# Two chained transformer blocks on one core: norms by halves, projection columns held on chip, eight buffers for raw weights

## The chip, the cores and the metric

The kernel runs on one core of a Trainium2 chip. The time is device microseconds of one execution; three runs of the kernel before took 1541.4 us in the median (1539.8 to 1542.86). Everything is one launch of a program of 23,433 instructions, without loops at run time.

## What is computed

Two blocks in a row on 256 tokens of width 1024 (`x`), the first with 256 context tokens beside them (`ctx`). The first block has two layers:

```
h  = rms(x)*g_pre*(1+sc1) + sh1 ;  hc likewise from ctx
u, uc = h @ w_in, hc @ w_in            # latent attention, short conv, bidirectional SSD scan
x  = x + g1 * rms(y @ w_out)*g_post     # y: the three mixers side by side
h2 = rms(x)*g_pre_ffn*(1+sc2) + sh2
x  = x + g2 * rms(relu(h2 @ w_ff1)**2 @ w_ff2)*g_post_ffn
# layer 0 does the last three lines for ctx too; layer 1 for x alone
```

The factors sh, sc, g come from `silu(c) @ w_mod`. The second block has two layers, one with dilated windowed attention (mixer a), one with a sliding window and sinks (mixer b):

```
h = mixer(x)                            # ends in  (o * silu(z)) @ w_out
x = layer_norm(sqrt(2)*x + h) * ln_g + ln_b
x = x + sigmoid(x @ ple_w_gate) * (p @ ple_w_proj)
```

All products are wanted in float32 accuracy.

## The kernel before

Tokens lie in four tiles of 128: tiles 2 and 3 are x (`X`), 0 and 1 the context (`CTX`). A tile `xt[t]` is two halves of 128x512. Every product is split by hand into float32r parts: an operand is a pair (high, low), and `mm3` issues three matmuls for each of the K blocks of 128 (high·high, high·low, low·high). A product of a token tile with 512 columns and K = 1024 is thus 24 matmuls of 128x512.

Weights come from memory block by block in `wblk` (L170): SP fetches 512 KB (two K blocks of 512 columns) into one of the five buffers of the ring `raw`; then `split` (L225) makes the pair, ACT by a cast (L226), DVE by a subtraction (L227), each on 128x512. The pairs lie in the rings `wh` and `wl` (ten slots each, so one block of eight K steps and two steps more), or, for the last `keep` K steps of a block, in two tiles of the general ring `u` (41 slots of 128x512, in which activations, layer outputs and x^T pairs lie too). A raw buffer comes free when its split is done.

Norms: `normed` (L400) squares each half of a tile on ACT with an accumulator, `rpow` (L164) takes the power -1/2 in two instructions on GpSimd (an add, L167, and a power, L168), and DVE scales both halves (L410). `modulated` (L414) then takes, for each of the eight K steps, PE transposes into a PSUM tile (two of those exist), a scale and shift on DVE (L424), an ACT cast of its result (L226) and a subtraction on DVE or GpSimd (L227). `postnorm` (L427) is the norm after a projection: square and gate product for each half once both halves are there, `rpow`, and x += on DVE (L435).

Order: the framework takes the instructions in the order of the program as their rank, plays a model of the engines, and lets each engine take the ready instruction with the best rank; `tc.high_priority(offset=n)` (and `sooner(n)`, L136) lifts what is inside by n ranks. So each engine has one fixed queue in the end, and the queues were interleaved by the model's times. All semaphores are made by the framework.

The stages, in order of time: the start with the first modulation; `mix(0)`; `out_projection(0)` (L881), which does the left 512 columns for all four tiles, then the right ones for X, the norm chain of X, then the right ones and the chain of CTX; `ffn(0)` (L903), eight steps of 512 hidden columns, of which the last is by token for X; `mix(1)`; `out_projection(1)`, x alone, with a chain for each tile; `ffn(1)`; `mixer_a`; `second(0)` (L1231): output projection by columns, layer norm and transposes by tiles (L1247), gate products; `mixer_b`; `second(1)`. `done` is the function by which each of these starts the norm and the modulation of what comes next; it does both at once. `load_cols(1)`, the masks and the rope tables of the second block are fetched by DMAs that GpSimd issues.

Of the kernel before, what the change touches and what calls it, by code (L numbers as in the profile page):

```python
# [16 lines left out]
P = 128  # L17
# [47 lines left out]
def body(ctx, tc, A, out):  # L65
# [8 lines left out]
    raw, wh, wl = pool("raw", 5), pool("wh", 10), pool("wl", 10)  # L74
# [89 lines left out]
    def rpow(out, a, b, eps):  # L164

        w = out.shape[1]
        POOL.tensor_scalar(out, a, eps if b is None else b, None if b is None else eps, ALU.add, *(() if b is None else (ALU.add,)))  # L167
        POOL.tensor_tensor(out, out, mhalf[:, 0:w], ALU.pow)  # L168
# [258 lines left out]
    def postnorm(t, halves, gate):  # L427

        s2, rs, r = S(2), S(1), [R(), R()]
        for hf in range(2):  # L430
            ACT.activation(R(), halves[hf], AF.Square, scale=1.0 / 32, accum_out=s2[:, hf:hf + 1])
            (DVE if hf else POOL).tensor_tensor(r[hf], halves[hf], gate[hf], ALU.mult)
        rpow(rs, s2[:, 0:1], s2[:, 1:2], EPS)
        for hf in range(2):
            DVE.scalar_tensor_tensor(xt[t][hf], r[hf], rs, xt[t][hf], ALU.mult, ALU.add)  # L435
# [44 lines left out]
    def mix(i, hT, W1, step):  # L480
# [389 lines left out]

        wuq = wsmall(A["w_uq"][i], 384, 2)
# [3 lines left out]
        if step is not None:  # L875
            parts["m"] = mods()
        interleaved(parts, "piiiilpdiiiiiiiseeeclcsccllssssazagzaga" if last
# [3 lines left out]
    def out_projection(i, ytok, done):  # L881

        gate = {r: mod_gate(i, 2, O_GQM, r) for r in ((0,) if i == 1 else (0, 1))}
        W = wblk(A["w_out"][i], [(0, 512)])
        if i == 0:
            for t in CTX:
                xt[t] = [U(), U()]
                load_x(t, SP)
        first = {}
        for t in X + (() if i else CTX):  # L890
            ps = AN()
            mm3(ps, list(zip(ytok(t), W)))
            first[t] = U()
            ACT.copy(first[t], ps)
        W = wblk(A["w_out"][i], [(512, 512)])
        for pair in ((X[0:1], X[1:2]) if i else (X, CTX)):
            for t in pair:
                ps = AN()
                mm3(ps, list(zip(ytok(t), W)))
                postnorm(t, [first[t], ps], gate[0 if t >= 2 else 1])  # L900
            done(pair)

    def ffn(i, h2, h2x, h2c, step, done):  # L903
# [3 lines left out]
        gate = {r: mod_gate(i, 5, O_GQF, r) for r in ((0,) if last else (0, 1))}  # L907
        for r_ in range(8):
            if r_ == 0 and last:

                nb = 2
                Ws = [wblk(A["w_ff1"][i], [(512 * q, 512)], keep=KT if q else 0) for q in range(nb)]
                first = {(t, q): (U(F32R), U(F32R)) for t in range(2) for q in range(nb)}
                for t in range(2):
                    for q in range(nb):
# [8 lines left out]
                        split(tp, *first[t, q])  # L924
            if last and r_ < nb:
# [15 lines left out]
            for (a, b), src in zip(parts, srcs):  # L941
                for ft in range(4):
# [8 lines left out]
                    if r_:  # L951
                        step(2)
            W7 = [wblk(A["w_ff2"][i], [(512 * n, 512)], 4 * r_, 4) for n in range(2)]
            for pair in (pairs if r_ == 7 else (sum(pairs, ()),)):
                by_token = r_ == 7 and pair == X
                for t, n in [(t, n) for t in pair for n in range(2)] if by_token else [(t, n) for n in range(2) for t in pair]:
# [8 lines left out]
                    else:  # L965
                        DVE.tensor_tensor(acc[t, n], acc[t, n], ps, ALU.add)
                    if r_ == 7 and n == 1:
                        postnorm(t, [acc[t, 0], acc[t, 1]], gate[0 if t >= 2 else 1])
                if r_ == 7:
                    done(pair)  # L970
# [22 lines left out]
    def xT():  # L993
# [3 lines left out]
        def fill(t):  # L997
            for j, pair in enumerate(tiles):
# [5 lines left out]
                split(tp[:, 0:256].rearrange("p (q c) -> p q c", q=2), h, l)  # L1004
# [14 lines left out]
    def load_mask(n):  # L1019
        m = C([P, 5, 256], "c_mask", BF16, tag="c_tri")[:, 0:4, :].rearrange("p (s a) c -> p s (a c)", s=2)  # L1020
        for s in range(2):
            r = R()
            POOL.dma_start(r, A[n][:, s * 512:(s + 1) * 512])
# [207 lines left out]
    def second(i, oT, pp, fill, done):  # L1231
        w_out = A["a_w_out_2" if i == 0 else "b_w_out_2"][0]
        lg, lb = [U(), U()], [U(), U()]
# [3 lines left out]
        st = [S(12), S(12)]  # L1237
        hT, transpose = xT()
        for n in range(2):
            W = wblk(w_out, [(512 * n, 512)])  # L1240
            for t in range(2):
                x = xt[2 + t]
                ps = AN()
                mm3(ps, tok(oT, t, W))
                DVE.scalar_tensor_tensor(x[n], x[n], ALPHA, ps, ALU.mult, ALU.add)
                DVE.bn_stats(st[t][:, 6 * n:6 * n + 6], x[n])
        for t in range(2):  # L1247
            x = xt[2 + t]
            mv, rs = S(2), S(1)
            DVE.bn_aggr(mv, st[t])  # L1250
            rpow(rs, mv[:, 1:2], None, LN_EPS)
            for n in range(2):
                DVE.scalar_tensor_tensor(x[n], x[n], mv[:, 0:1], lg[n], ALU.subtract, ALU.mult)
                DVE.scalar_tensor_tensor(x[n], x[n], rs, lb[n], ALU.mult, ALU.add)
            transpose(t)
        W = [wblk(A["ple_w_gate_2"][i], [(512 * n, 512)], keep=(0 if n else KT)) for n in range(2)]
        got = None
        for t in range(2):
            x = xt[2 + t]
            for n in range(2):  # L1260
# [3 lines left out]
                ACT.activation(e, ps, AF.Tanh, scale=0.5)  # L1264
                DVE.scalar_tensor_tensor(e, e, 1.0, pp[t][n], ALU.add, ALU.mult)
                DVE.tensor_tensor(x[n], x[n], e, ALU.add)
                if i == 1:
                    SP.dma_start(out[0, t * P:(t + 1) * P, 512 * n:512 * n + 512], x[n])
            done(t)
            if t == 0:  # L1270
                got = fill()
        return got
# [97 lines left out]
```

## Time and profile before

| | before |
|---|---|
| median of 3 runs | 1541.4 us |
| profiled execution, its own time | 1537.98 us |
| its span, first to last instruction | 1535.9 us |
| mean granted TensorE clock | 0.986 |
| HBM read | 233.87 MB, 153 GB/s over the span |

The profile is that of one execution. Matmuls are pipelined, so their busy time (PE) is not the same as PE at its peak; the pace of back-to-back matmuls is read from the chain of waits. PEclk is the granted clock of TensorE as a share of 2.4 GHz; its two levels are 1.2 and 2.4 GHz. "<-" behind an idle time names what ended it.

### The profile page before, as it was taken

How to read it: one execution, taken by the hardware profiler on the slowest of the kernel's cores; microseconds unless marked ns; L12 is line 12 of the kernel's file. 1: busy time of each engine (PE TensorE's matmuls, PEld its weight loads, DVE VectorE, ACT ScalarE, POOL GpSimd, SP SyncE). 2: the span in 40 equal slices, each digit the busy share in tenths (PEclk: the TensorE clock that was granted, in tenths of full speed). 3: DMA queues.
4: the chain of work that ended last, by engine and by line, in shares of the span. 5: the costliest groups of instructions: out<-in, count | busy, mean ns of one | idle time of the engine just before them, and what ended most of it. 6: DMA issues, size and time to landing. Idle time of an engine off the chain costs nothing.

```text
span 1535.9 us, 23433 instructions
## 1 busy us (share of the span) xinstructions
PE 1470.2 (96%) x8417; PEld 1215.3 (79%) x8417; DVE 1036.4 (67%) x2057; ACT 740.4 (48%) x1594; POOL 308.2 (20%) x356
## 2 busy tenths in 40 slices
PE   6997999999999999998899899999999999999998
PEld 4766678888878888878797689997888889878886
DVE  3559556478597557478776756676876786567866
ACT  3433345564233333255556654565566457445663
POOL 1225201150001111034331301112310320021110
PEclk9998999999999999999999999999999999999999
DMA  9854622325366546334423546555436550645442
GB/s 294 266 182 153 219 84 88 97 66 195 123 219 206 180 152 200 109 83 135 132 76 117 165 139 213 188 195 169 153 107 203 162 179 15 219 139 180 138 149 69
DMA packets 131687, 236.51 MB, mean 154 GB/s; under 512 B 12624, under 2 KB 31251, under 8 KB 131571
## 3 DMA queue, kind: packets, MB, share of 16 engines
q1 hardware_dynamic: 130688, 233.46, 47.0%
q0 software_dynamic: 704, 1.50, 0.3%
q8 instruction: 66, 1.08, 0.3%
q14 instruction: 50, 0.41, 0.1%
q10 hardware_dynamic: 179, 0.06, 0.0%
HBM read 233.87 MB, written 1.11 MB: 153 GB/s over the span
## 4 chain that ended last, share of the span: by engine, by line
PE 84%; DVE 7%; DMA 4%; issue 2%; ACT 2%; POOL 1%; SPq 0%; ACTq 0%; DVEq 0%; POOLq 0%
PE sc L212 47%; PE mm L212 20%; PE tp L459 3%; DVE wl L227 2%; PE fl L303 2%; DMA raw<-in_w_mod_dram 1%; DMA raw<-in_ple_w_gate_dram 1%; PE fl L212 1%; DMA raw<-in_w_in_dram 1%; PE sc L793 1%; PE mm L639 1%; PE sc L1083 1%; PE sc L634 1%; DVE u L782 1%; PE sc L1108 1%
## 5 line engine op out<-in xcount | busy, mean ns | idle before, releaser
L227 DVE TENSOR_TENSOR wl<-raw,wh 128x512 fp32r<-128x512 f32 (+1 forms) x606 | 421.2, 731 | 141.1 <-ACT wh L226 138.1
L226 ACT CAST wh<-raw 128x512 fp32r<-128x512 f32 (+1 forms) x606 | 359.2, 620 | 307.0 <-PE sc L212 104.5
L212 PE MATMUL sc<-wh,u 128*128 128x512 f32 (+2 forms) x1424 | 458.6, 389 | 3.5 <-DVE r L505 2.0
L212 PEld LDWEIGHTS sc<-wh,u 128*128 128x128 f32 x1424 | 265.4, 189 | 58.8 <-ACT p L226 2.2
L212 PE MATMUL sc<-wl,u 128*128 128x512 f32 (+2 forms) x712 | 274.6, 387 | 0.1
L212 PE MATMUL sc<-u,wh 128*128 128x256 f32 (+1 forms) x1072 | 265.1, 336 | 1.8 <-ACT wh L226 1.1
L212 PE MATMUL mm<-wh,u 128*128 128x512 f32 (+1 forms) x648 | 219.3, 395 | 1.0 <-ACT u L226 1.0
L212 PEld LDWEIGHTS sc<-u,wh 128*128 128x128 f32 x1072 | 184.0, 191 | 24.5 <-issue 2.0
L212 PE MATMUL sc<-u,wl 128*128 128x256 f32 (+1 forms) x536 | 178.0, 335 | 0.0
L212 PEld LDWEIGHTS sc<-wl,u 128*128 128x128 f32 x712 | 134.6, 189 | 24.8 <-DVE wl L227 0.5
L949 POOL TENSOR_TENSOR r<-r 128x256 f32<-128x256 f32 (+1 forms) x60 | 64.3, 1073 | 420.1 <-ACT r L947 380.2
L212 PEld LDWEIGHTS mm<-wh,u 128*128 128x128 f32 x648 | 122.2, 190 | 26.1 <-ACT u L226 1.7
L212 PE MATMUL mm<-wl,u 128*128 128x512 f32 (+1 forms) x324 | 127.2, 393 | 0.0
L212 PE MATMUL mm<-u,wh 128*128 128x256 f32 (+1 forms) x512 | 117.6, 317 | 1.1 <-ACT wh L226 1.0
L212 PEld LDWEIGHTS sc<-u,wl 128*128 128x128 f32 x536 | 102.0, 191 | 9.6
L342 DVE SCALAR_TENSOR_TENSOR q<-raw,c_sT,q 128x512 f32<-128x512 f32 x112 | 85.0, 788 | 13.8 <-DMA raw<-in_w_mod_dram 13.2
L212 PEld LDWEIGHTS mm<-u,wh 128*128 128x128 f32 x512 | 86.1, 191 | 9.2 <-issue 1.7
L212 PE MATMUL mm<-u,wl 128*128 128x256 f32 (+1 forms) x256 | 80.4, 314 | 0.0
L950 DVE TENSOR_TENSOR u<-r,u 128x256 fp32r<-128x256 f32 (+1 forms) x60 | 33.6, 561 | 63.0 <-POOL r L949 60.7
L1016 POOL TENSOR_TENSOR r<-r,r 128x512 f32<-128x512 f32 (+1 forms) x30 | 44.6, 1491 | 151.4 <-DVE r L1014 151.3
L212 PEld LDWEIGHTS mm<-wl,u 128*128 128x128 f32 x324 | 61.5, 190 | 12.5 <-issue 0.8
L227 POOL TENSOR_TENSOR u<-r,u 128x256 fp32r<-128x256 f32 (+1 forms) x48 | 38.2, 801 | 119.3 <-ACT u L226 119.0
(318 smaller groups left out, 1984.7 us busy)
## 6 DMA issues: line engine op xcount, KB each, us to landing
raw<-in_w_ff_dram SPq DMA_DIRECT2D x128, 512.0 KB, 4.5
raw<-in_w_mod_dram SPq DMA_DIRECT2D x80, 512.0 KB, 4.5
raw<-in_a_w_in_dram SPq DMA_DIRECT2D x80, 512.0 KB, 3.9
raw<-in_w_in_dram SPq DMA_DIRECT2D x32, 512.0 KB, 5.1
raw<-in_b_w_in_dram SPq DMA_DIRECT2D x18, 512.0 KB, 4.6
raw<-in_w_mod_dram SPq DMA_DIRECT2D x32, 256.0 KB, 5.2
raw<-in_w_out_dram SPq DMA_DIRECT2D x16, 512.0 KB, 3.8
raw<-in_ple_w_gate_dram SPq DMA_DIRECT2D x16, 512.0 KB, 3.9
```

Of the source, the lines that this page charges most:

```text
L212: PE.matmul(ps, s, m, start=(i == 0), stop=(i == n - 1))
L226: ACT.copy(h, src)
L227: (eng or DVE).tensor_tensor(l, src, f(h), ALU.subtract)
L303: PE.matmul(ps[32 * g:32 * g + 32, :], sT[:, k + q, :], rs[g // per][:, q, w * (g % per):w * (g % per) + w], start=(k + q == 0), stop=(k + ...
L342: DVE.scalar_tensor_tensor(a, r[:, q, :], w, a, ALU.mult, ALU.add)
L459: PE.transpose(tp[:, b * P:(b + 1) * P], p[:, b * P:(b + 1) * P], ident)
L634: PE.matmul(ps[:, b * P:(b + 1) * P], qT[t][:, hs], kT[b][:, hs], start=True, stop=True, skip_group_check=True)
L639: PE.matmul(po[64 * e:64 * e + 64, hp * P:(hp + 1) * P], V[b // 2][:, 256 * (b % 2) + 64 * h:256 * (b % 2) + 64 * h + 64], pT[e][:, b * P: ...
L782: DVE.tensor_scalar(o, o, cs[:, t, c:c + 1], 0.0, ALU.subtract, ALU.min)
L949: POOL.tensor_tensor(f2[:, a:b], r[:, a:b], r[:, a:b], ALU.mult)
L950: DVE.tensor_tensor(l, f2[:, a:b], f(h), ALU.subtract)
L1016: POOL.tensor_tensor(a[:, 0:w], a[:, 0:w], b[:, 0:w], ALU.add)
```

## The change

- `raw` has eight buffers, not five. The scratch for DMAs issued by GpSimd is cut to 1024 bytes; all DMAs that GpSimd issued (`load_cols(1)`, masks, rope tables) are issued by ACT.
- `rpow` does its add on DVE; the power stays on GpSimd.
- `modulated`: ACT makes the high part itself from PSUM (scale and shift in the activation), beside DVE's float32 result; both and the subtraction are lifted by 300.
- `postnorm` is a function that is called for each half as it comes, lifted by 300. In `out_projection` it reads the product in PSUM, so the copy of the left halves (L894) is gone.
- `done` now starts the norm alone and gives back a function that does the modulation; the callers run it later: X's after CTX's products, CTX's inside `ffn`'s first step, or in `mix(1)` between the projections of X and of CTX (part "m"); in layer 1, that of tile 3 after tile 2's first products in `ffn(1)`.
- `out_projection(1)`, `ffn(1)` and `second` go tile by tile over both column blocks, in the order (0,1) for the first tile and (1,0) for the second; one block lies in `u` (keep=KT), one in `wh` and `wl`.
- `second`: layer norm chain lifted by 300, transposes moved behind the projections of both tiles; ln_g and ln_b lie in the ring `q`; `ple(1)` is issued whole after the first tile's gates.

```diff
-    raw, wh, wl = pool("raw", 5), pool("wh", 10), pool("wl", 10)
+    raw, wh, wl = pool("raw", 8), pool("wh", 10), pool("wl", 10)
@@ rpow
-        POOL.tensor_scalar(out, a, eps if b is None else b, ...
+        DVE.tensor_scalar(out, a, eps if b is None else b, ...
         POOL.tensor_tensor(out, out, mhalf[:, 0:w], ALU.pow)
@@ modulated
-            DVE.tensor_scalar(r[:, 0:w], tp[:, 0:w], a, b, ALU.mult, ALU.add)
-            split(r[:, 0:w], h, l, POOL if k % 2 else DVE)
+            with tc.high_priority(offset=300):
+                ACT.activation(h, tp[:, 0:w], AF.Identity, bias=b, scale=a)
+                DVE.tensor_scalar(r[:, 0:w], tp[:, 0:w], a, b, ALU.mult, ALU.add)
+                (POOL if k % 2 else DVE).tensor_tensor(l, r[:, 0:w], f(h), ALU.subtract)
@@ postnorm
+    def postnorm(t, gate):
+        s2, rs, r = S(2), S(1), {}
+        @sooner(300)
+        def half(hf, src, o, eng):
+            r[hf] = o
+            ACT.activation(R(), src, AF.Square, scale=1.0 / 32, accum_out=s2[:, hf:hf + 1])
+            eng.tensor_tensor(o, src, gate[hf], ALU.mult)
+            if len(r) == 2:
+                rpow(rs, s2[:, 0:1], s2[:, 1:2], EPS)
+                for q in range(2):
+                    DVE.scalar_tensor_tensor(xt[t][q], r[q], rs, xt[t][q], ALU.mult, ALU.add)
+        return half
@@ out_projection
+        W.append(wblk(A["w_out"][i], [(512, 512)], keep=KT if i else 0))
+        half = {t: postnorm(t, gate[0 if t >= 2 else 1]) for t in X + (() if i else CTX)}
+        end = None
+        def product(t, n):
+            ps = AN()
+            mm3(ps, list(zip(ytok(t), W[n])))
+            half[t](n, ps, U(), DVE)
+        if i == 0:
+            for t in X + CTX:
+                product(t, 0)
         for pair in ((X[0:1], X[1:2]) if i else (X, CTX)):
             for t in pair:
+                for n in (1,) if i == 0 else (1, 0) if end else (0, 1):
+                    product(t, n)
+            new = done(pair)
+            if end:
+                end()
+            end = new
+        return end
@@ ffn
-                Ws = [wblk(A["w_ff1"][i], [(512 * q, 512)], keep=KT if q else 0) for q in range(nb)]
+                Ws = [wblk(A["w_ff1"][i], [(512 * q, 512)], keep=0 if q else KT) for q in range(nb)]
...
-                    for q in range(nb):
+                    for q in (1, 0) if t else (0, 1):
...
+                    if t == 0:
+                        end()
...
+                if r_ == 0 and src is h2x and not last:
+                    end()
...
+                    with tc.high_priority(offset=300 if r_ == 7 else 0):
                         DVE.tensor_tensor(acc[t, n], acc[t, n], ps, ALU.add)
+                    if r_ == 7:
+                        if n == 0:
+                            half[t] = postnorm(t, gate[0 if t >= 2 else 1])
+                        half[t](n, acc[t, n], R(), DVE if n else POOL)
                 if r_ == 7:
-                    done(pair)
+                    new = done(pair)
+                    if later:
+                        later()
+                    later = new
+        return later
@@ mix: "piiiilpdiiii..." becomes "piiiilmpdiiii...", in layer 1 "m" is the function given back by ffn(0)
@@ second
+        W = [wblk(w_out, [(512 * n, 512)], keep=KT if n else 0) for n in range(2)]
+        lg, lb = [Q(), Q()], [Q(), Q()]
...
         for t in range(2):
             x = xt[2 + t]
+            for n in (1, 0) if t else (0, 1):
+                ps = AN()
+                mm3(ps, tok(oT, t, W[n]))
+                with tc.high_priority(offset=300):
+                    DVE.scalar_tensor_tensor(x[n], x[n], ALPHA, ps, ALU.mult, ALU.add)
+                    DVE.bn_stats(st[t][:, 6 * n:6 * n + 6], x[n])
             ...                       # bn_aggr, rpow, 4 scalar_tensor_tensor, lifted by 300
         W = [wblk(A["ple_w_gate_2"][i], [(512 * n, 512)], keep=(0 if n else KT)) for n in range(2)]
         for t in range(2):
+            transpose(t)
+            for n in (1, 0) if t else (0, 1):
...
@@ body
     def mid0(pair):
-        modulated(normed(pair), ...)
+        xn = normed(pair)
+        return lambda: modulated(xn, ...)
-    pp = second(0, oT, pp, late, transpose)
+    pp = second(0, oT, pp, lambda: ple(1)(), transpose)
```

## Rows read from the trace of the kernel before

**Rows 1.** The page: busy us of each engine, share, instructions

```profile
PE 1470.2 (96%) x8417; PEld 1215.3 (79%) x8417; DVE 1036.4 (67%) x2057; ACT 740.4 (48%) x1594; POOL 308.2 (20%) x356
```

**Rows 2.** Windows: stretch, width, busy by engine (count), granted clock, DMA share, GB/s

```profile
335.00:655.00 320.00, 319.91 (x1438) 258.89 (x1437) 214.10 (x337) 109.22 (x192) 38.64 (x31) 1.00 0.52 169
320.00:330.00 10.00, 6.74 (x38) 5.26 (x37) 8.00 (x18) 4.28 (x12) 4.31 (x7) 0.83 0.00 0
675.00:685.00 10.00, 7.60 (x38) 5.65 (x38) 8.37 (x16) 2.56 (x7) 2.35 (x3) 1.00 0.42 104
695.00:715.00 20.00, 16.33 (x106) 14.39 (x104) 17.44 (x43) 11.96 (x34) 9.07 (x12) 0.91 0.61 184
850.00:870.00 20.00, 14.51 (x56) 10.03 (x56) 15.80 (x34) 11.26 (x30) 8.09 (x11) 0.91 0.41 129
1045.00:1055.00 10.00, 7.57 (x28) 5.54 (x27) 6.91 (x11) 4.34 (x11) 6.77 (x9) 0.86 0.50 158
1370.00:1380.00 10.00, 6.59 (x30) 4.34 (x29) 8.99 (x19) 4.37 (x10) 3.12 (x5) 1.00 0.42 139
1500.00:1510.00 10.00, 8.56 (x33) 6.27 (x32) 8.80 (x17) 3.19 (x8) 3.40 (x4) 0.83 0.34 105
100.00:150.00 50.00, 39.98 (x242) 28.70 (x236) 42.10 (x112) 18.84 (x45) 31.30 (x39) 0.86 0.53 175
```

**Rows 3.** Waits of PE: total us, times, longest

```profile
PE tp L420 <- DVE q L410: 7.0, 4, 3.2
PE fl L303 <- DMA raw<-in_w_mod_dram: 3.8, 5, 2.0
```

**Rows 4.** Chain of waits, 355 to 380 us: start, length, what

```profile
363.04 10.88 PE sc L212 x48
```

**Rows 5.** Timeline around the first layer's output projection: start, length, what

```profile
306.57 0.40 PE L212 MATMUL sc<-wh,u 128*128 128x512 f32 x1
311.64 0.63 ACT L431 ACTIVATE r<-u 128x512 f32<-128x512 f32 x1
322.53 0.88 DVE L410 TENSOR_SCALAR q<-u,s 128x512 f32<-128x512 f32 x2 [0.69 <-POOL s L168]
```

**Rows 6.** Timeline of the second layer's output projection

```profile
849.73 0.39 PE L212 MATMUL sc<-wh,u 128*128 128x512 f32 x1
853.30 0.41 PE L420 MATMUL tp<-c_ident,q 128*128 128x128 f32 x2 [3.19 <-DVE q L410]
854.55 0.77 PE L212 MATMUL sc<-wh,u 128*128 128x512 f32 x1
```

**Rows 7.** Groups of instructions: busy us, mean ns, idle before

```profile
L227 DVE TENSOR_TENSOR wl<-raw,wh 128x512 fp32r<-128x512 f32 (+1 forms) x606 | 421.2, 731 | 141.1 <-ACT wh L226 138.1 <-PE sc L212 2.3
L435 DVE SCALAR_TENSOR_TENSOR x<-r,s,x 128x512 f32<-128x512 f32 x16 | 11.3, 747 | 3.7 <-POOL s L168 3.7
L406 ACT ACTIVATE r<-x 128x512 f32<-128x512 f32 x16 | 10.1, 629 | 4.0 <-DVE x L435 2.6 <-DMA x<-in_x_dram 1.3
L168 POOL TENSOR_TENSOR s<-s,c_mhalf 128x1 f32<-128x1 f32 (+1 forms) x44 | 32.7, 743 | 2.8
L167 POOL TENSOR_SCALAR s<-s 128x1 f32<-128x1 f32 (+1 forms) x44 | 22.3, 506 | 144.5 <-DVE s L1250 44.8 <-ACT r L854 37.6 <-ACT r L431 25.0
```

**Rows 8.** Timelines: a small DVE operation, DMA issues of ACT and GpSimd

```profile
4.93 0.18 DVE L280 TENSOR_SCALAR c_sT<-tp 128x16 f32<-128x16 f32 x1 [0.45 <-PE tp L279]
3.06 0.57 ACTq L254 DMA_DIRECT2D r<-in_g_pre_mix_dram  x1
1047.58 1.17 POOL L1023 DMA_DIRECT2D r<-in_mask_a_dram  x2
```

**Rows 9.** Waits of SP's queue, and a DMA issue with KB and us to landing

```profile
SPq L180 <- DVE wl L227: 723.0, 229, 30.8
u<-csT SPq DMA_DIRECT2D x24, 256.0 KB, 3.4
```

More of the change, by code (lines that the diff above doesn't have):

```diff
@@ L869, in mods, with rest @@
                 yield
+        def rest():
+            step()
+            yield
         wuq = wsmall(A["w_uq"][i], 384, 2)
@@ L874, in mix @@
                  "s": short(), "z": zgates(), "c": scans(), "g": gated_norm()}
-        if step is not None:
-            parts["m"] = mods()
-        interleaved(parts, "piiiilpdiiiiiiiseeeclcsccllssssazagzaga" if last
+        parts["m"] = rest() if last else mods()
+        interleaved(parts, "piiiilmpdiiiiiiiseeeclcsccllssssazagzaga" if last
                     else "ppmiidiiiieeelmcccccmmmmlcmcmllsaasasasaaczsaszgzagzgg")
@@ L952, in ffn @@
                         step(2)
+                if r_ == 0 and src is h2x and not last:
+                    end()
             W7 = [wblk(A["w_ff2"][i], [(512 * n, 512)], 4 * r_, 4) for n in range(2)]
             for pair in (pairs if r_ == 7 else (sum(pairs, ()),)):
-                by_token = r_ == 7 and pair == X
-                for t, n in [(t, n) for t in pair for n in range(2)] if by_token else [(t, n) for n in range(2) for t in pair]:
+                half = {}
+                for t, n in [(t, n) for t in pair for n in range(2)] if r_ == 7 else [(t, n) for n in range(2) for t in pair]:
                     ps = AN()
@@ L1022, in load_mask @@
             r = R()
[L1023 removed]
+            ACT.dma_start(r, A[n][:, s * 512:(s + 1) * 512])
             POOL.tensor_copy(m[:, s, :], r)
@@ L1294, in body @@
     SP.dma_start(tri, A["tri"])
-    cols[1], halves[1] = load_cols(1, POOL)
+    cols[1], halves[1] = load_cols(1, ACT)
     yT = mix(0, hT, W1, mod_units((0, 1), (0, 2)))
@@ L1313, in end0 @@
             mod_scale(1, 1, O_GPM, a=sc1)
-        modulated(normed(pair), 0 if pair == X else 1, sc1, mods[1][:, 0:8, :], hx if pair == X else hc)
-    ffn(0, h2, h2x, h2c, step, end0)
-    yT = mix(1, hT, None, None)
+        xn = normed(pair)
+        return lambda: modulated(xn, 0 if pair == X else 1, sc1, mods[1][:, 0:8, :], hx if pair == X else hc)
+    end = ffn(0, h2, h2x, h2c, step, end0, end)
+    yT = mix(1, hT, None, end)
     h2 = [U(F32R) for _ in range(KT)]
@@ L1338, in step @@
             first.append(ple(0))
-    ffn(1, None, h2x, None, step, lambda pair: None)
+    ffn(1, None, h2x, None, step, lambda pair: None, end)
     pp = first[0]()
     oT = mixer_a()
-    late = ple(1)
     hT, transpose = xT()
-    pp = second(0, oT, pp, late, transpose)
+    pp = second(0, oT, pp, lambda: ple(1)(), transpose)
     second(1, mixer_b(hT), pp, lambda: None, lambda t: None)
```

83 lines of the change are left out of this document (28 added, 55 removed).

## The prediction

> **What bounds it now.** The page's busy times are read first: PE is busy for 96% of the span, the engines that feed it for 67% and less [rows 1], so only time in which PE waits or runs slowly can be won. Next the table of windows by stage. In the feed-forward of layer 0 (335 to 655) PE is busy for 319.91 of 320 us at full clock, and the chain of waits shows its pace there: 48 matmuls of 128x512 in 10.88 us, 0.227 us each, so 5.44 us for a product of 24 [rows 2, 4]. Nothing is to be had in such stretches, however late a weight is. What is lost lies in seven short windows, each at a place where a norm stands between two projections [rows 2]. In each I count the width less PE's busy time, plus the busy time times (1 - granted clock):
>
> - 320 to 330, layer 0 after its output projection: 3.26 + 0.17 x 6.74 = 4.4
> - 675 to 685 and 695 to 715, layer 0 to layer 1: 2.40, and 3.67 + 0.09 x 16.33 = 5.1
> - 850 to 870, layer 1 after its output projection: 5.49 + 0.09 x 14.51 = 6.8
> - 1045 to 1055, into mixer a: 2.43 + 0.14 x 7.57 = 3.5
> - 1370 to 1380 and 1500 to 1510, the two layer norms of the second block: 3.4, and 1.44 + 0.17 x 8.56 = 2.9
>
> The sum is 28.5 us, of which some 22 are idle and 6.5 are time at the lower of the two clock levels (1.2 GHz) behind an idle stretch: the clock costs where PE has just waited. PE's waits name the end of these gaps: 7.0 us in four waits of the transposes (L420) for DVE's last norm step (L410) [rows 3]. The timelines show why the chain ends late. In layer 0 the last product with 512 columns starts at 306.57, but ACT squares the context's first half, long finished, only at 311.64, and DVE's last scaling starts at 322.53 [rows 5]: the chain waited behind the modulation of X and behind halves taken together. In layer 1 only one product (5.44 us) lies between tile 2's last half and its transposes; PE stops after 849.73 for 3.19 us [rows 6].
>
> **What the change does to this, part by part.** PE's own work stays: same products, same transposes.
>
> Norm by halves, lifted. After the last product there remain for one tile: a square 0.63, the add 0.18 (a small DVE operation; it was 0.51 on GpSimd), the power 0.74, x += twice 0.75, two squares 1.26, add and power 0.92, two scalings of about 0.75 at most [rows 7, 8]: 6.7 us, some 7.5 with hops, against 16.4 from 306.97 to 323.41 for the two context tiles now. What covers it: for X in both layer changes of block 1, the context's products (10.9 us: two of 5.44, or four of half the K in the feed-forward); for the context, the first features or the projection of X, no less than 9 us; in layer 1 and in both layer norms, two products instead of one (10.9 us). All covers exceed 7.5, so the waits for L410 go, and with them the slow clock behind them.
>
> What is late next. With the modulation moved behind the covering products, PE comes to transposes whose input is ready, but the first product behind them must wait for the first modulated pair. The nearest rows: transposes at 853.30, first matmul at 854.55, 1.25 us [rows 6]; with ACT and DVE working side by side it may be a little less, with 256 columns a little more, so 1.4. It occurs at most eleven times (twice at each of the five places with two chains, once into mixer a). Four of the second ones have ready work for PE beside them (the products of X's first hidden block, `mix`'s next parts, the first tile's second-stage products, `ple(1)`). Seven are left: 7 x 1.4 = 9.8 us. Bounds: none of them exposed gives 28.5 of gain, all eleven 28.5 - 15.4 = 13.1. I take 28.5 - 9.8 = 18.7, because the greedy queue fills with whatever is ready but has nothing behind X's chain.
>
> Both blocks held. The number of splits stays (one of DVE takes 0.731 [rows 7]); only where they wait changes. In `second`, the ring `u` then holds 8 tiles of o^T, 16 of the kept block, 8 of x^T and 4 of the embedding product: 36 of 41, so two K steps of the gate's kept block can be split ahead, and two of the other in `wh`; 12 of 16 remain when the second tile's products begin. Until the second gate product ends there are four products, 21.8 us, in which DVE also carries two chains of six operations of 0.75 (9.0 us): 12.8 us or 17 splits of room for 12. Cost nothing, margin five splits; if that margin is gone, see the third rival.
>
> Eight raw buffers. SP's queue waits 723 us in total for splits to free a buffer [rows 9], but PE's matmuls wait for a fetch for 3.8 us only, in five waits, all on w_mod [rows 3]. I take 1.5 us of the 3.8; bounds 0 and 3.8. A rule of the Trainium skill speaks against deeper prefetch ("DMA: Bandwidth & Descriptors", Queues, rings and completion order): on each DMA engine the descriptors of one queue are consumed in the order of its ring, so small loads on SP stand behind three more fetches. The trace has 3.4 us from issue to landing for the scan's rows u<-csT, of half a fetch's size [rows 9], so no such delay is seen at five buffers; by row I count nothing, by rule it is the fourth rival.
>
> The rest. `rpow`'s add moved to DVE saves 0.3 us on a chain and costs DVE 44 x 0.18 = 8 us of its 500 idle ones [rows 1, 7, 8]. The exception is 100 to 150 in `mix(0)`, where DVE is busy for 42 of 50 and PE loses 10.0 + 0.14 x 39.98 = 15.6 us [rows 2]: there the change may gain or lose some; nearest bounds are four adds of 0.18 lost in a row and 4 x 0.51 gained, doubled for reordering, -4 to +2; I take 0. Issues moved from GpSimd to ACT: 14, of 0.3 to 0.6 us [rows 8], 4 to 8 us of ACT's 795 idle ones, and 1.17 us for two of them leave GpSimd just where the norm into mixer a needs it. What stands behind them on ACT is casts of weights that are ahead of PE. Nothing.
>
> **The sum.** 18.7 + 1.5 = 20 us off the profiled execution's 1537.98, so 1518; the median of the runs shown is 3.4 us higher, so 1521.4.
>
> **Rivals.**
>
> 1. The gaps only change their shape: all eleven restarts are exposed and each queue, made from modelled times, misses a cover or two. For it: the context's chain lost 16.4 us in a queue that the model had also ordered [rows 5]. Against it: covers of 9 to 11 us for 7.5. Gain 4 to 11: about 1534. Within 3 us of the old time if the order before was as good as any: 1541.
> 2. More than the gaps: the lifted chains and deeper prefetch also clear part of `mix(0)`'s 15.6 and of the start. Against it: DVE, not weights, is full there. Gain 28 to 45: about 1505.
> 3. Slower. In `ffn(1)` and both `second`, the weight splits come late: if all sixteen splits of the two next blocks are left when the second tile's last product begins, DVE has 9.0 us of chains and 11.7 us of splits, 20.7, against three products, 16.3 us: PE waits 4.4 us and then loses another 1.4 at the lower clock, with two restarts of 1.25. That is 8.3 a place, 24.9 at three, where 13.1 are lost now; and with lifted norms the same crowding eats the gain at the two places of layer 0 (DVE is busy for 8.0 of 10 us there and 17.4 of 20 [rows 2]). 1538 + 11.8 - 2 (into mixer a) = 1548, plus 3.4: 1551. It decides from ten splits left (16.3 - 9.0 = 7.3 us of room). By my count 12 are left when the product before begins, and the kept block's tiles come free in it one K step at a time, so ten or fewer: close.
> 4. The ring order: three fetches of 512 KB at the 175 GB/s of 100 to 150 [rows 2] are 9 us more before a row of decays lands. With three of the scan's six tiles exposed: 27 us lost against 20 won, 1548.
>
> That the change does nothing of what it says (the queues come out in the old order) is in the 1541 of the first.
>
> **How the numbers follow.** Forecast (gain 12 to 28) 0.52; rival 1 with a gain 0.15, without one 0.08; rival 2 0.13; rival 3 0.08; rival 4 0.04. A measurement of this kernel tells 0.2%, 3.1 us, from no change. Faster: 0.52 + 0.15 + 0.13 = 0.80; same 0.08; slower 0.12. The forecast's own range is 1513 to 1529; the range for 8 in 10 goes from 1503 (half of rival 2) to 1543 (all of rival 1).
>
> **What would show it.** Right: in the windows of the seven places, PE idle of 1 to 3 us each, the clock at 1.00 in most; no wait of L420's transposes for L410 of over 1 us, but waits of about 1 us of the first product for the first modulated pair (ACT's high part or the subtraction); ACT's square right behind each left product. Eight buffers: SP's wait for splits falls, PE's matmuls unchanged in count. Wrong: matmuls after a norm waiting for `wl` or for DVE's weight subtraction (rival 3); the scan's matmuls waiting for rows of csT (rival 4); or idle time in the seven windows near 22 us still. The prediction is wrong at its root if the time changes mainly in stretches between the seven places.

## The result: 3.85% slower, and the profile after

| | before | after |
|---|---|---|
| median, measured side by side | 1541.27 us | 1600.08 us |
| profiled execution, its own time | 1537.98 us | 1605.07 us |
| its span | 1535.9 us | 1603.3 us |
| mean granted TensorE clock | 0.986 | 0.967 |

The ratio is 1.0385, with a 95% interval from 1.0358 to 1.0413. I had forecast a gain of 20 us; the change loses 59. DVE and ACT are busy for 9 us more than before and GpSimd for 41 less [rows 1]; PE has the same 8417 matmuls, but is busy with them for 23.8 us longer and idle for 43.6 us longer. First the page's busy times, then windows of the kernel after (columns as in [rows 2]):

```profile
PE 1494.0 (93%) x8417; PEld 1229.7 (77%) x8417; DVE 1045.0 (65%) x2107; ACT 749.5 (47%) x1588; POOL 267.6 (17%) x292
```

```profile
60.00:76.00 16.00, 9.27 (x30) 6.46 (x29) 7.93 (x27) 8.05 (x19) 2.36 (x4) 0.70 0.68 232
326.00:336.00 10.00, 4.98 (x25) 4.02 (x24) 9.74 (x22) 6.22 (x16) 3.23 (x4) 0.83 0.63 203
715.00:727.00 12.00, 3.35 (x15) 2.70 (x14) 11.02 (x22) 6.30 (x18) 6.63 (x6) 0.78 0.60 169
900.00:912.00 12.00, 6.98 (x18) 4.76 (x19) 8.55 (x23) 6.40 (x18) 2.58 (x6) 0.61 0.00 0
1563.00:1575.00 12.00, 6.97 (x25) 5.09 (x24) 11.97 (x24) 2.36 (x5) 1.97 (x2) 0.72 0.00 1
```

The four lower ones are places of the prediction: PE is idle for 5 to 9 us of 10 to 12, where it idled for 1.4 to 5.5 in the windows there before [rows 2], and the granted clock, a mean of 1.2 and 2.4 GHz, is lower in each but one; DVE is full in three. The first is a new place. PE's waits, as in [rows 3]:

```profile
PE tp L420 <- DVE r L426: 12.0, 3, 7.2
PE sc L800 <- DVE u L795: 7.9, 5, 3.5
PE tp L1034 <- DVE x L1287: 7.6, 2, 5.0
PE sc L212 <- ACT wh L226: 6.7, 1, 6.7
PE tp L420 <- DVE q L410: 6.2, 1, 6.2
PE sc L708 <- DVE c_la L705: 4.9, 1, 4.9
```

The 7.0 us in four waits for the norm (L410) are 6.2 in one. Beside it stand a wait for the modulation's scale (L426), one for the layer norm's last step (L1287), one for weight casts and one in `mix(1)`. The scan's waits for DVE's products (L795) were 1.1 us in one before; the longest of the five now, 3.5 us, ends at 185.7, where DVE does two weight splits from 183.09 to 184.99 ahead of a product whose inputs are there by 182.9.

To place the loss I took, for each profiled execution, the time at which PE begins its nth microsecond of matmul work (each at its back-to-back pace, 0.227 us for 512 columns), minus that of the kernel before. Its growth by stage, in us:

```
                                start+mix0  out0-ffn0  ffn0  ffn0-mix1  mix1  out1-ffn1  both second  all
after                                 20.5        8.6   7.1        4.6   6.3        9.0         11.5   67
eight buffers + ACT's issues           9.3       -0.1   4.6        0.7   0.2        1.5         -0.1   15
eight buffers only                     1.7        0.0   4.4        1.7  -1.9        2.9         -2.1    6
ACT's issues only                      8.0       -0.2   0.5       -1.5   0.2       -0.8          0.5    5
modulation only (ACT's high part)      8.4        3.3   1.5        6.9  -0.4        0.3         -0.2   20
  the same, DVE ahead of ACT           2.6        1.9   1.0        6.1  -1.9        3.2         -0.2   13
  its lift only                        4.1        0.2   1.2       -1.6  -1.4        0.6         -0.2    1
DVE's add in the power only            5.1       -0.8   1.0        1.8   3.5        3.8          0.6   15
halves and DVE's add                   9.6        1.5   0.4        3.5   3.8        3.0          1.8   24
halves and the lift, GpSimd's add      7.3       -1.9   0.7        0.1  -1.5        0.6          0.1    4
tile 3 first and the lift              4.0        0.0   0.9       -1.5  -1.2       -1.9          0.1    1
after, five buffers                    9.9        3.2   1.7       17.4  10.0       15.1         10.8   68
after, modulation ahead of the norm   17.9        7.1   5.4        9.7   5.3        5.7          8.9   58
after, nothing postponed              16.8        0.8   5.6        3.5  -0.5        4.7         11.8   43
after, old second stages              16.2        6.8   8.2        5.8   6.0        8.7         -0.3   51
after, tile 3 first                   18.6        7.5   5.8        5.9   6.0        4.9         11.8   60
parts that help                        5.2       -1.9   0.6       -0.1   0.2       -2.0          0.3    2
  and the layer norm's lift            2.9       -1.3   0.9        1.5  -1.2       -2.6         -0.2   -1
```

These are single executions ("all" is against a profile of before 3 us under its median, and the profile of the kernel after lies 5 us over its own, so that 59 us become 67), and the first 60 us scatter: the last two kernels, alike there, differ by over 2 us. Half of the loss, 34 of 67 us, lies at the places of the prediction, half between them, where I had named a change as a sign that its root is wrong.

### The profile page after: what moved, and what is told of

Its sections match the earlier page's. It is cut to its first block, busy times and chain, and to the rows that moved or that the text cites. A ratio compares the mean times of both kernels' runs of the same rounds, so it can differ in the third digit from the quotient of the medians.

```text
span 1603.3 us, 23384 instructions
## 1 busy us (share of the span) xinstructions
PE 1494.0 (93%) x8417; PEld 1229.7 (77%) x8417; DVE 1045.0 (65%) x2107; ACT 749.5 (47%) x1588; POOL 267.6 (17%) x292
## 4 chain that ended last, share of the span: by engine, by line
PE 73%; DVE 10%; DMA 4%; issue 2%; ACT 2%; POOL 1%; DVEq 0%; ACTq 0%; POOLq 0%
PE sc L212 41%; PE mm L212 18%; DMA raw<-in_w_mod_dram 3%; PE tp L466 3%; DVE wl L227 2%; DVE q L342 1%; PE sc L800 1%; PE sc L1116 1%; PE mm L646 1%; PE fl L212 1%; PE sc L641 1%; PE sc L1141 1%; PE fl L303 1%; DVE u L227 1%; PE tp L420 1%
## 5 line engine op out<-in xcount | busy, mean ns | idle before, releaser
L227 DVE TENSOR_TENSOR wl<-raw,wh 128x512 fp32r<-128x512 f32 (+1 forms) x582 | 405.4, 731 | 119.4 <-ACT wh L226 115.6
L226 ACT CAST wh<-raw 128x512 fp32r<-128x512 f32 (+1 forms) x582 | 348.1, 620 | 272.4 <-PE sc L212 136.7
L212 PE MATMUL sc<-wh,u 128*128 128x512 f32 (+2 forms) x1344 | 439.3, 393 | 8.4 <-DVE u L973 2.7
L212 PEld LDWEIGHTS sc<-wh,u 128*128 128x128 f32 x1344 | 252.8, 190 | 65.5 <-DVE u L973 4.0
L212 PE MATMUL sc<-u,wh 128*128 128x256 f32 (+1 forms) x1072 | 272.5, 340 | 9.6 <-ACT wh L226 6.7
L212 PE MATMUL sc<-wl,u 128*128 128x512 f32 (+2 forms) x672 | 260.3, 389 | 0.3 <-DVE wl L227 0.3
L212 PEld LDWEIGHTS sc<-wl,u 128*128 128x128 f32 x672 | 128.5, 191 | 23.9 <-DVE wl L227 0.8
L212 PE MATMUL mm<-u,wh 128*128 128x256 f32 (+1 forms) x512 | 124.3, 321 | 1.4 <-ACT u L425 1.4
L212 PE MATMUL sc<-u,u 128*128 128x512 f32 (+1 forms) x282 | 77.1, 402 | 0.3 <-ACT u L226 0.2
L168 POOL TENSOR_TENSOR s<-s,c_mhalf 128x1 f32<-128x1 f32 (+1 forms) x44 | 31.8, 723 | 226.5 <-DVE s L167 226.5
```

The costliest lines, as they stand in the source:

```text
L212: PE.matmul(ps, s, m, start=(i == 0), stop=(i == n - 1))
L226: ACT.copy(h, src)
L227: (eng or DVE).tensor_tensor(l, src, f(h), ALU.subtract)
```

## The experiments

All are told as medians with the kernel before run beside them (1540.6 to 1541.4 us).

**The buffers.** Eight buffers and ACT's issues alone on the kernel before; the reverse (five buffers and GpSimd's issues in the changed kernel); then each half alone.

```diff
-    raw = pool("raw", 5)                       # eight buffers (and scratch 1024)
+    raw = pool("raw", 8)
-    cols[1], halves[1] = load_cols(1, POOL)    # ACT's issues (masks and rope tables too)
+    cols[1], halves[1] = load_cols(1, ACT)
```

> The kernel before with the buffer part of the change alone: eight raw buffers, the small scratch, and the fourteen DMAs of GpSimd issued by ACT. Theory 1 (ACT's queue is blocked at the start, because each of its eight column loads waits for a completion that the large fetches of SP hold): the loss of the changed kernel's first 220 us, about 20 us, is here too, and nothing else, so about 1561 us, with ACT's casts standing still until about 69 us. Rival (the losses all come from the norms and their order): within 3 us of 1541.

> The changed kernel with the buffer part undone: five raw buffers, the usual scratch, the fourteen DMAs issued by GpSimd again. Theory 1: the 20 us of the first 220 us come back and the losses at the norms stay, about 1580 us. Rival (the norms' order costs it all, the buffers are neutral): 1597 to 1603. Second rival (eight buffers fill the model's queues so that the norms come out badly too): under 1565.

> The kernel before with eight raw buffers and the small scratch, the fourteen DMAs still issued by GpSimd. Theory 1 (ACT's issues cost the start, deeper prefetch costs the feed-forward of layer 0 through DVE's waits for w_mod): the first 200 us as before, 4 to 6 us lost in the feed-forward, 1545 to 1548 us. Rival (the buffers cost both): 1551 to 1556, as with ACT's issues.

> The kernel before with five buffers, but the fourteen DMAs issued by ACT. Theory 1: the loss of the first 200 us is here, up to 9 us, none in the feed-forward: 1546 to 1550 us. Rival (with five buffers fewer fetches are under way, so ACT's issues are never held up): within 2 us of 1541.

Together: 1553.29 us, ratio 1.009 (1.0074 to 1.0106), 12.5 of the 20 us that theory 1 put on them. Eight buffers only: 1544.44, 1.0025 (1.0011 to 1.0039). ACT's issues only: 1544.01, 1.0019 (0.9999 to 1.004). So each costs about 3 us and both 12.5, and theory 1 placed them rightly: ACT's issues in the first 200 us, also with five buffers, the buffers in the feed-forward of layer 0. That the two together cost more than their sum was not taken apart. The reverse gave 1602.27: nothing comes back in all, the rival's number but not its reason, since the first 200 us gain 11 us, layer 0's output projection 5 and its feed-forward 5, and the change of layer, `mix(1)` and layer 1's output projection lose 23 more. The new order is better off with eight buffers there; why was not tried further.

How ACT's issues cost shows the timeline of the kernel after:

```profile
59.73 0.41 ACTq L254 DMA_DIRECT2D r<-in_b_mod_dram  x1
61.13 0.28 ACTq L254 DMA_DIRECT2D r<-in_g_post_mix_dram  x1
66.16 0.28 ACTq L254 DMA_DIRECT2D r<-in_g_pre_ffn_dram  x1
69.27 0.31 ACTq L254 DMA_DIRECT2D r<-in_ssd_conv_b_dram  x1
69.62 2.70 ACT L226 CAST wh<-raw 128x512 fp32r<-128x512 f32 x5 [5.10 <-DMA r<-in_g_post_ffn_dram]
70.29 2.08 PE L212 MATMUL sc<-u,wh 128*128 128x512 f32 x4 [6.73 <-ACT wh L226]
```

An issue takes 0.3 to 0.4 us, but eight take from 59.73 to 69.6. By the trace's semaphores each but the first waits for one of eight counters of landed transfers, which all transfers issued by SP and ACT share in turn: the issue at 66.16 has the counter of a fetch of 512 KB that SP issued at 59.3, and waits until that has landed. The casts that PE wants stand behind it. In the kernel before, GpSimd's issues of the same loads had counters of their own and waited for no landing. With eight buffers more of SP's fetches can be under way; that this is why the two parts together cost more is not shown. In the feed-forward it is DVE that waits, here with eight buffers only (before, the first of these was 13.2 us in 7 waits):

```profile
DVE q L342 <- DMA raw<-in_w_mod_dram: 39.2, 12, 4.5
DVE q L340 <- DMA raw<-in_w_mod_dram: 12.5, 8, 3.1
```

The queues were made from modelled landings; with deeper prefetch DVE meets w_mod ahead of its landing, and behind that wait stands the low part of the squares of the hidden features (L950), for which PE waits there for 2.1 us in two waits; before it had none there.

**The modulation.** ACT's own high part with the lift on the kernel before; the lift alone; and the same with DVE's scale written ahead of ACT's reading.

```diff
+            with tc.high_priority(offset=300):                      # lift
+                ACT.activation(h, tp[:, 0:w], AF.Identity, bias=b, scale=a)   # behind the next line in the third
                 DVE.tensor_scalar(r[:, 0:w], tp[:, 0:w], a, b, ALU.mult, ALU.add)
-            split(r[:, 0:w], h, l, POOL if k % 2 else DVE)          # kept where the lift is alone
+                (POOL if k % 2 else DVE).tensor_tensor(l, r[:, 0:w], f(h), ALU.subtract)
```

> The kernel before with only the modulation changed: ACT makes the high part from PSUM beside DVE, both lifted by 300. Theory (this is the part that slows the first 220 us, since lifted modulation steps stand ahead of the weight splits there): 1548 to 1552 us. Rival (it is neutral or gains 0.5 us on each of the places): 1535 to 1541.

> The kernel before with only the lift by 300 around the modulation's scale and split; ACT casts DVE's result as before. Theory 5 (what costs 8 us in the first 220 us and 10 at the two layer changes with the modulation alone is that DVE's scale waits for ACT's reading of the same PSUM tile, so the tile is held by two operations of 0.55 us in a row, not by one): within 4 us of 1541. Rival (the lift puts modulation ahead of weight splits that PE wants sooner): 1549 to 1555.

> The kernel before with ACT's own high part and the lift, as in the run with the modulation alone, but with DVE's scale written ahead of it, so that of the two readers of one PSUM tile ACT waits for DVE. Theory 5a (the 18 us come from DVE, whose queue is full, standing still for ACT): 1539 to 1546 us, DVE's scale without a wait for ACT. Rival 5b (they come from the PSUM tile being held through two readings, whichever is first): 1549 to 1556.

1552.63 us (1.0077, 1.0056 to 1.0098); lift alone 1539.62 (0.999, 0.9972 to 1.0008); DVE ahead 1552.13 (1.008, 1.0065 to 1.0096). So the lift costs nothing that these runs can tell, and ACT's reading 11 to 13 us. The groups of the scale, first in the kernel after, then with DVE ahead (busy, mean ns, idle before):

```profile
L425 ACT ACTIVATE u<-tp,c_mod,c_scale 128x256 fp32r<-128x256 f32 (+1 forms) x64 | 33.2, 536 | 46.2 <-PE tp L420 39.5 <-DVE c_scale L380 6.4
L426 DVE TENSOR_SCALAR r<-tp,c_scale,c_mod 128x256 f32<-128x256 f32 (+1 forms) x64 | 32.1, 508 | 31.1 <-ACT u L425 30.8
```

```profile
L426 ACT ACTIVATE u<-tp,c_mod,c_scale 128x256 fp32r<-128x256 f32 (+1 forms) x64 | 33.3, 537 | 48.0 <-DVE r L425 47.6
L425 DVE TENSOR_SCALAR r<-tp,c_scale,c_mod 128x256 f32<-128x256 f32 (+1 forms) x64 | 31.3, 508 | 17.4 <-PE tp L420 16.7
```

The two do not work side by side: in either order none of the 64 pairs overlaps, whichever comes second begins when the other has ended, though both only read. The Trainium skill says so ("PSUM — Partial Sum Buffer", PSUM bank collisions raise a hardware error): two engines may not reach the same bank and partitions at once, reads against reads included, so the compiler's scheduler puts a dependency between them. The trace agrees, with 30.8 us of DVE's idle time behind ACT, where the scale waited 7.0 us in all before. By the medians rival 5b has the right number: turning the order round gives nothing back. Its reason, the tile held through two readings (1.14 us in the median, where one reading took 0.51), is shown for one order alone: at the change of layer, where both lose 6 to 7 us, PE's transposes wait for ACT's reading for 4.4 us with DVE ahead, but with ACT ahead PE waits for ACT's weight casts (3.6 us in two waits). ACT's queue, in which the reading takes 0.54 us where the cast took 0.38, is a rival that no run parts from it. The profiles put 6 us of difference into the first 200 us, but the first one is the slowest of its four runs, so whether DVE's waiting plays a part there stays open.

**The norm by halves and DVE's add.** Both on the kernel before; these and the modulation; the add alone; halves with the lift but GpSimd's add.

```diff
-        POOL.tensor_scalar(out, a, ...)                 # the add
+        DVE.tensor_scalar(out, a, ...)
-                postnorm(t, [first[t], ps], gate)       # halves: half[t](0, ps, ...) at the first product
+                half[t](1, ps, U(), DVE)
```

> The kernel before with the norm after a projection by halves, lifted, and DVE's add in the power; the modulation as before. Theory 5 (the halves themselves gain, ACT's high part took it back): 1530 to 1538 us, with the gaps of 3.3 us after layer 0's output projection and 3.2 us in layer 1 shorter. Rival (a chain that is ready sooner is not what the gaps hang on, the rest of the queue is): 1539 to 1545.

> The kernel before with only the norms' inner part: DVE's add in the power, ACT's own high part and the lift in the modulation, the norm after a projection by halves and lifted. No postponing, no kept blocks, five buffers, old DMAs. Theory (the norms by halves gain what was forecast in part, the rest of the change eats it): 1525 to 1538 us, the square of the first half right behind its product. Rival (the same lifts cost 10 us in the first 220 us, as in the changed kernel with five buffers): 1545 to 1552.

> The kernel before with the add of the power on DVE alone. Theory 6 (in mix(0), where DVE is full, and at each norm the add waits in DVE's queue for its input and holds up what stands behind it; this is what the norm by halves paid in the first 200 us and in mix(1)): 1548 to 1556 us, 8 to 10 of them before 200 us. Rival (44 adds of 0.2 us are nothing, the halves' lifts displaced the rest): 1539 to 1543.

> The kernel before with the norm by halves and the lift of the modulation, but GpSimd's add and ACT's cast of DVE's result as before. Theory 6: without DVE's add the first 200 us cost no more than with the lift alone (4 us), and the halves gain 1 to 3 us at the output projection of layers 0 and 1: 1536 to 1541. Rival (the halves displace the weight splits whoever adds): 1546 to 1556.

1561.05 us (1.012, 1.0089 to 1.015), 1557.45 (1.011, 1.009 to 1.013), 1553.4 (1.0093, 1.0078 to 1.0108) and 1539.95 (0.9998, 0.9987 to 1.001). The first two are slower than either expectation had them: halves and add together cost 20 us, 7 more than the add alone, which is not explained. The add, 44 times 0.19 us, costs 13 us, and the halves without it nothing (they gain 1.9 us after layer 0's output projection, none in layer 1); theory 6 holds, but with 5 us before 200 us, not 8 to 10, and 9 from the layer change on. Where it happens shows `mix(0)`, first with the add alone, then before:

```profile
123.75 0.19 ACT L559 ACTIVATION_READ_ACCUMULATOR p<-u 128x1 f32 x1
130.07 0.16 DVE L167 TENSOR_SCALAR s<-s 128x2 f32<-128x2 f32 x1
130.69 0.69 POOL L168 TENSOR_TENSOR s<-s,c_mhalf 128x2 f32<-128x2 f32 x1
```

```profile
123.38 0.19 ACT L559 ACTIVATION_READ_ACCUMULATOR p<-u 128x1 f32 x1
123.66 0.38 POOL L167 TENSOR_SCALAR s<-s 128x2 f32<-128x2 f32 x1 [1.11 <-ACT p L559]
124.13 0.71 POOL L168 TENSOR_TENSOR s<-s,c_mhalf 128x2 f32<-128x2 f32 x1
```

On idle GpSimd the add starts 0.09 us after its input; on DVE it stands 6.1 us behind scan work. Over all 44 the way from input to power shrinks from 1.9 to 1.7 us in the mean: the mean gains what I said, the one late chain costs it.

**The postponed modulation.** In the changed kernel, first ahead of the next norm and lifted by 600, then not postponed.

```diff
-            new = done(pair)          # first: end() ahead of done(pair), modulation lifted by 600
-            if end: end()
+            if end: end()
+            end = done(pair)
-        xn = normed(pair)             # second: at once
-        return lambda: modulated(xn, ...)
+        modulated(normed(pair), ...)
+        return lambda: None
```

> The changed kernel with the postponed modulation issued ahead of the next norm and lifted by 600, not 300, so that on DVE the modulation of X no longer stands behind the context's norm chain. Theory 3 (that order is what makes PE wait at the two layer changes of block 1): the waits of 3.7 and 7.2 us for the first modulated pair go, and with them most of the 8.5, 5.3 and 7 us lost after them, so 1580 to 1587 us. Rival (postponing itself costs it: whichever chain is second is now late, PE waits for the context's modulation in its place): 1597 to 1605.

> The changed kernel with the modulation straight behind its norm again (nothing postponed), all else as changed. Theory 3b (postponing is what costs at the layer changes of block 1: the second chain then stands before or behind the first modulation on one DVE queue): the 8.5, 5.3 and 7 us lost after the output projection and the feed-forward of layer 0 and in mix(1) go, about 1580 us, or less if layer 1 gains too. Rival (the lifts of the norms alone do it): 1595 to 1605.

1598.5 us (1.0394, 1.0365 to 1.0423) and 1578.51 (1.0249, 1.0229 to 1.0268). The order of the two chains is not it (the waits for L426 fall from 12.0 to 5.2 us, but the two changes and `mix(1)` lose 22 us where they lost 20); postponing is: 22 us come back, by the profiles 16 where theory 3b said and 4 in layer 1. The kernel after, at the change from layer 0 to 1 (start, length, what):

```profile
714.59 0.60 PE L420 MATMUL tp<-c_ident,q 128*128 128x128 f32 x4
714.76 3.36 POOL L437 TENSOR_TENSOR r<-u,q 128x512 f32<-128x512 f32 x1 [2.17 <-DVE s L167]
719.12 1.41 DVE L441 SCALAR_TENSOR_TENSOR u<-r,s,u 128x512 f32<-128x512 f32 x2 [0.44 <-POOL s L168]
722.52 1.41 DVE L441 SCALAR_TENSOR_TENSOR u<-r,s,u 128x512 f32<-128x512 f32 x2 [0.54 <-POOL s L168]
723.85 0.88 DVE L410 TENSOR_SCALAR q<-u,s 128x512 f32<-128x512 f32 x2
724.64 0.54 DVE L426 TENSOR_SCALAR r<-tp,c_scale,c_mod 128x256 f32<-128x256 f32 x1
725.24 0.69 PE L420 MATMUL tp<-c_ident,q 128*128 128x128 f32 x2 [7.17 <-DVE r L426]
```

X's first transposes are done at 715.2; their scale on DVE comes at 724.64, behind the whole norm chain of the context, which itself waits for GpSimd twice. Both PSUM tiles are full, PE stands. Not postponed, PE's wait for it is gone (0.5 us left of 12.0); the wait for L410 is not (6.2 us with it):

```profile
PE tp L420 <- DVE r L426: 0.5, 2, 0.3
PE tp L420 <- DVE q L410: 7.6, 3, 5.9
```

**Both column blocks, tile by tile.** In the changed kernel the second block's stages as they were (which also takes back their lifts, the later transposes, the place of ln_g and ln_b and `ple(1)` issued whole); tile 3 ahead of tile 2 in layer 1; the latter, with the lift, on the kernel before.

```diff
-        for pair in ((X[0:1], X[1:2]) if i else (X, CTX)):     # tile 3 first
+        for pair in ((X[1:2], X[0:1]) if i else (X, CTX)):
-                    for q in (1, 0) if t else (0, 1):          # and in ffn(1): t in (1, 0)
+                    for q in (0, 1) if t else (1, 0):
```

> The changed kernel with the second block's projections in the old order (by columns, no kept block, no lifts). Theory 2 (tile by tile over two kept blocks the queue spends the covering product early, and weight splits stand between the steps of the chain): the 12 us lost in the two output stages of the second block come back, about 1588 us. Rival (these places lose because of the deeper prefetch, or of DVE's add): 1597 to 1603.

> The changed kernel with tile 3 ahead of tile 2 in the output projection of layer 1 and in the first products of its feed-forward. Theory 4 (attention leaves tile 3's inputs ready first, so with both column blocks on chip PE takes tile 3's products early and nothing covers tile 2's chain): of the 9 us lost there most comes back, 1590 to 1594 us. Rival (not the order of tiles but the splits or the lifted chain): 1597 to 1603.

> The kernel before with the lift alone and tile 3 ahead of tile 2 in the output projection of layer 1 and the first products of its feed-forward. Theory 4 (tile 3's inputs are ready first, so its product is used up early and covers nothing): the wait of 3.2 us there falls to under 1 us, 1535 to 1539 us. Rival (tile 3's chain is as late when it is first): within 2 us of 1541.

1589.72 us (1.0324, 1.0309 to 1.034): the 11.8 us lost in the two stages come back, as theory 2 said. 1597.5 (1.037, 1.035 to 1.039): by the profiles 4 of 9 us at layer 1, though the median, 2.6 us lower, lies within the runs of the kernel after (1597.63 to 1605.07). 1538.52 (0.999, 0.9981 to 0.9999): 2 us there, but not by the way I named, since the wait for L410 stays 3.2 us. The kernel after in layer 1, where tile 2's last product is the last that PE has:

```profile
895.73 1.52 PE L212 MATMUL sc<-u,u 128*128 128x512 f32 x6
897.29 0.60 ACT L436 ACTIVATE r<-sc 128x512 f32<-128x512 f32 x1 [3.11 <-PE sc L212]
901.56 0.58 ACT L436 ACTIVATE r<-mm 128x512 f32<-128x512 f32 x1
903.49 0.66 PE L420 MATMUL tp<-c_ident,q 128*128 128x128 f32 x2 [6.24 <-DVE q L410]
```

Attention leaves tile 3 ready first. Before, half of one of its products had been run early: behind tile 2's last there were 12 matmuls of 24 up to the wait of 3.19 us [rows 6]. With both blocks on chip both products were, squared only at 901.56, and tile 2's chain of 6.2 us, 1.3 less than I said, has no cover at all. With tile 3 first the wait for L410 is gone there. In `second(1)` of the kernel after:

```profile
1558.54 0.61 PE L212 MATMUL sc<-u,u 128*128 128x512 f32 x2
1559.84 1.89 DVE L227 TENSOR_TENSOR u<-raw,u 128x512 fp32r<-128x512 f32 x3
1561.65 0.68 DVE L1279 SCALAR_TENSOR_TENSOR x<-x,sc 128x512 f32<-128x512 f32 x1
1565.11 0.39 PE L212 MATMUL sc<-wh,u 128*128 128x512 f32 x1
1570.49 1.12 PE L1034 MATMUL tp<-c_ident,x 128*128 128x128 f32 x4 [4.99 <-DVE x L1287]
```

The first tile's product ends at 1559.2, but PE had mixed it with the kept block's other one, so only 6 us of work are left behind it; and DVE, which has the next block's splits in its queue, takes 2.5 us to begin the chain and 11.3 to end it.

**What is left to gain.** The kernel before with halves, lift (not at the start) and tile 3 first; then the layer norm lifted too, by columns as before.

```diff
+            with tc.high_priority(offset=300):       # in second, around L1244 and the layer norm
```

> The kernel before with the three parts that did not lose in the runs so far: the norm after a projection by halves, the modulation's lift (not at the start), and tile 3 first in layer 1. GpSimd's add, ACT's cast, five buffers and GpSimd's DMAs stay, nothing is postponed. Theory (the parts add up where they act: 1.9 after layer 0's output projection, 3 at the change of layer, 2 in layer 1): 1533 to 1537 us. Rival (each of them only reshuffled the queues, gains of 2 us do not add): 1538 to 1542.

> The same, and in the second block's output stages the layer norm's operations lifted by 300, by columns as before. Theory (there it is the kept blocks that cost 11 us, not the lift): 1 to 3 us below the run with the parts that help. Rival (the lift is what cost there): 3 to 11 us above it.

1536.07 us (0.9965, 0.995 to 0.9981) and 1535.1 (0.9956, 0.9943 to 0.997): both beat the kernel before. The lift of the layer norm costs nothing, so the 11 us lost in `second` come from the rest of what was changed there: the two kept blocks taken by tile, as the timeline above has it, or one of the smaller changes, which no run undoes by itself. The last kernel's waits for the norms are 5.6 us for L410 where before had 7.0 [rows 3], and 0.6 for the layer norm, where before had 0.7 and the same kernel without this lift 1.7:

```profile
PE tp L420 <- DVE q L410: 5.6, 3, 3.2
PE tp L1011 <- DVE x L1265: 0.6, 1, 0.6
```

## Why the prediction was wrong

The bottleneck was read rightly, and the last two runs show that it gives something at the places named; the price list failed.

- *"All covers exceed 7.5, so the waits for L410 go."* I counted covers (PE's work left while a chain runs) in the program's order. In the queue the covering product of layer 1 was spent before the chain began (cover 0, chain 6.2; in the kernel before, 12 matmuls were left of the 24 that I read there), and in `second(1)` the cover was 6 us for a chain of 11.3. In block 1's layer changes they went, and the wait for the modulation came instead.
- *Seven restarts of 1.4 us.* Three waits of together 12.0 us: I looked at PE for what is late next, not at DVE, where the postponed scale and the other norm's chain stand in one queue. In the kernel after the scale is second there and late; with the order turned the waits for it fall to 5.2 us, other waits take their place, and the time stays. By the runs postponing is the largest step, 22 us.
- *"With ACT and DVE working side by side."* They take turns; 11 us alone, though how they cost it is shown in part only.
- *The add: 0.3 us saved, DVE has 500 idle us; -4 to +2 in `mix(0)`.* Idle time on the average is not idle time where the add stands: 13 us alone, 5 of them in the first 200 us.
- *ACT's issues: "Nothing", eight buffers +1.5.* I counted the issues' durations and not what each waits for, nor that DVE meets the transfers too: 12.5 us together.
- *"Both blocks held: cost nothing."* 10.4 us in the second block's stages and part of 9 at layer 1. The third rival had the right places, and a growth of 11.8 us there (24.9 less the 13.1 lost before) against 20.5 measured, but another sign: no matmul waited for `wl` there, the chain itself stood behind splits. I gave it 0.08.
- The fourth rival's sign is not there: no wait for the scan's rows (u<-csT) stands among the waits of any engine. The scan's matmuls do wait longer, 7.9 us for 1.1, but for DVE's products.

The single parts, each alone or undone alone, come to 22 + 13 + 12.5 + 11 + 10 + 3 = 71 us for 59 lost; they overlap, and the runs do not part them further.

## What to carry to other kernels

The price of an instruction moved to another in-order engine, or of a DMA issued from it, is what stands ahead of it and behind it there, so read that queue at the place where it lands, not the engine's idle share. A product covers a chain only if the queue still has it when the chain begins: look which one PE ends with, above all after giving it more that is ready. Several edits of one idea are best run one by one; here what helped of it, with tile 3 first added, was worth 5 us, and the rest cost over 60.

## What was not expected of the hardware

GpSimd's product of 128x512 in the norm (L437) took 1.29 to 1.30 us in all twelve cases before, and 1.30 to 3.36 in the six of the kernel after. The longest [above, 714.76] ran while DVE did four subtractions with two inputs without a pause from 714.66 to 717.0; less 1.3 us, it begins where they end. The kernel before has the like in the feed-forward of layer 1: GpSimd's product of 128x256 (L949) takes 0.61 us by itself, and 1.98 to 2.06 us in five of its 32 places, where subtractions on DVE follow one another from before its start to 1.5 us behind it:

```profile
940.26 0.61 POOL L949 TENSOR_TENSOR r<-r 128x256 f32<-128x256 f32 x1 [2.28 <-ACT r L947]
942.88 3.69 DVE L227 TENSOR_TENSOR wl<-raw,wh 128x512 fp32r<-128x512 f32 x6
944.98 2.06 POOL L949 TENSOR_TENSOR r<-r 128x256 f32<-128x256 f32 x1 [4.11 <-ACT r L947]
```

The product at 944.98 ends at 947.04, 0.5 us after the last subtraction. That fits the Trainium skill ("SBUF — State Buffer", SBUF: two separate sides), by which a DVE operation with two inputs from SBUF and a GpSimd one that reads there lock each other out for a whole instruction; here GpSimd stays out through three in a row. What it costs the kernel was not tried by itself.
